# Hybrid decoder layer: attention values as the stationary operand, results by features, sample key sums in four column groups

## Chip, cores and metric

The kernel runs on one core of one Trainium2 chip. The metric is the device time of one execution in microseconds. The core's engines are named as the profile names them: PE is TensorE (matmuls; PEld is its weight load), DVE is VectorE, ACT is ScalarE, POOL is GpSimd, SP is SyncE, which here issues DMAs.

## The reference

One layer of a decoder trunk and a last norm, for a prompt of 512 tokens and 8 sample sequences of one token each, which share the weights. Cut to what matters here:

```
u = RMSNorm(x)
[qA,kA,vA | qB,kB,vB,rB,gate_lowrank | gate_A,gate_B] = u @ w_in
A: dilated sliding-window softmax attention, 3 head groups x 4 heads x 64 dims,
   (window, dilation) = (128,1),(512,4),(2048,16); for each head slot the three groups' outputs
   are merged, weighted by their softmax denominators -> 256 wide
   samples: one query against the cached keys and values of each group
B: gated linear attention (GLA), 4 heads, dk=128, dv=256:
   S_t = diag(a_t) S_{t-1} + k_t^T v_t, o_t = q_t S_t, RMSNorm per head, swish gate -> 1024 wide
mix = sigmoid(gate_A) * (oA @ w_pa) + sigmoid(gate_B) * (oB @ w_pb);   x = x + mix @ w_o
x = x + relu(RMSNorm(x) @ w_up)^2 @ w_down
```

Of the change only two pieces of A are touched: the products of probabilities and values of the prompt, with the merge of the groups, and the sum over cached positions of probabilities times values of the samples.

## The kernel before

Activations are kept by features: 128 features on the partitions, 520 columns for 512 prompt tokens and 8 samples, in two halves of 260. The weights come in panels of 1024 x 128. Each panel is loaded by SP (`raw`), split by ACT into a rounded high part (`whi`, L90) and by DVE into the rest (`wlo`, L91); two half panels each, four buffers. The panel loop (L124, tile `mps`) multiplies high by high, high by low and low by high: 8 slices x 3 passes x 2 halves, 48 matmuls of 128 x 128 by 260. Most of PE's time is this loop, through the panels of w_in, w_pa (2), w_pb, w_o, w_up and w_down.

Everything else is filler between the panels. The parts are generators: prompt attention (`attn`, from L311), the samples' attention (`attn_s`, L402), the GLA heads of the prompt (`gla`, L548), and the samples' states (`gla_s`, L662). Between two panels `fill` (L130) advances them by one to four steps, and at the end `finish` (L143) drains what is left. GLA's generators begin only when both attention generators are done (`gla_parts`, L828). The order in which the instructions come out of this is then arranged by the framework's scheduler with a timeline of its own, so a change in one filler moves others. All fillers share four PSUM banks (`bank`, L66).

*Prompt attention* works through two sides, the direct group (`on`) and the two dilated groups (`oc`), each in four blocks of 128 queries. A block computes scores (`sps`, L332), exponentials (L340) with their minima and sums in `stN` and `stC`, transposes of the probabilities (`ptp`, L347), and their product with the values (`pvp`, L358). In that product the transposed probabilities are the stationary operand, 128 x 128, and 64 columns of values of one head move; the result stands by tokens. At the end, the weights of the two sides are worked out from exchanged minima and sums (`cz`, L375 to L383), the two results are multiplied by them (L385), transposed to features (`oT`, L391 and L396) and added into `oa` (L393, L398).

*Samples' attention* multiplies the cached values by the probabilities in place (`kcb`, L472), adds the groups, and sums over the 128 cached positions on the partitions (`spO`): 16 matmuls with a 128 x 128 piece of `kcb` as the stationary operand and a single column of ones moving. They are put on a list (`small_mm`, L154) and taken from it between the steps of the panel loop or by `finish` (L151). DVE then copies the result (L484).

*A GLA head* computes decays (`zp`, L554), scaled keys and their transposes (`klp`, L575, copied by ACT as `klT`, L577), then six levels of a triangular product (`lev`, L545, L610, L615) whose factors `D` take two exponentials on ACT each (L604, L605) and have three buffers, then POOL's copies into `ST` (L626), the state matmuls (`gpo`, `gpu`, L632 to L636), a norm, and transposes of the result (`gop`, L656). The samples' states are loaded in pairs, split by ACT and POOL into high and low (L701, L702) and multiplied (`gso`, L706).

Behind the panels of the two gates, ACT computes their sigmoids over all 4160 columns at once (gA at L871, gB at L872), with a table load before and behind. Then come the two w_pa panels (stationary w_pa, moving `oas`) and the w_pb panels, which need the GLA result split into `obh` and `obl` (L741).

Of the kernel before, what the change touches and what calls it, by code (L numbers as in the profile page):

```python
# [9 lines left out]
F32 = mybir.dt.float32  # L10
F32R = mybir.dt.float32r
U8 = mybir.dt.uint8
AF = mybir.ActivationFunctionType
ALU = mybir.AluOpType
# [4 lines left out]
D = 1024  # L19
S = 512  # L20
NB = 8
P = 128
HC = 260
NT = 2 * HC
# [6 lines left out]
def pv(t):  # L31

    return t[:, :, :256]
# [11 lines left out]
class Build:  # L45
# [265 lines left out]
    def attn(self, ap):  # L311
        nc = self.nc
        on, oc, prTs = self.on, self.oc, self.prTs
        stN = ap.tile([P, 4, 2, 4], F32, tag="stN", name="stN", bufs=1)
        stC = ap.tile([P, 4, 2, 4], F32, tag="stC", name="stC", bufs=1)
        K, Q, V = self.KTt, self.QTt, self.Va
        for side, (o, st, mk) in enumerate(((on, stN, self.c["maskN"]), (oc, stC, self.c["maskC"]))):
            while side == 1 and self.groups_ready < 3:
                yield True
            for b in range(4):  # L320
                first = 1 if side == 0 and b == 0 else 0
                pss = [self.bank("sps").rearrange("p (h x) -> p h x", h=2) for _ in range(2)]
                for hp in range(2):
                    for hh in range(2):
                        rows = slice(64 * hh, 64 * hh + 64)
                        if side == 0:
                            nc.tensor.matmul(pss[hh][:, hp, first * P:], Q[rows, hp, b * P:(b + 1) * P],
                                             K[rows, hp, (b - 1 + first) * P:(b + 1) * P], start=True, stop=True)
                        else:
                            for gg in range(2):  # L330
                                i = 2 + 2 * gg + hp
                                nc.tensor.matmul(pss[hh][:, hp, gg * P:(gg + 1) * P], Q[rows, i, b * P:(b + 1) * P],  # L332
                                                 K[rows, i, b * P:(b + 1) * P], start=True, stop=True)
                prs = [ap.tile([P, 2, 256], F32, tag="pr", name="pr", bufs=3) for _ in range(2)]
                for h in range(4):
                    pr = prs[h // 2]
                    nc.vector.tensor_tensor_reduce(
                        pr[:, h % 2, first * P:], pss[h % 2][:, h // 2, first * P:], mk[:, first * P:], scale=-0.125,
                        scalar=3.0e38, op0=ALU.add, op1=ALU.min, accum_out=st[:, b, 0, h:h + 1])
                    nc.scalar.activation(pr[:, h % 2, first * P:], pr[:, h % 2, first * P:], AF.Exp, scale=-1.0,  # L340
                                         bias=st[:, b, 0, h:h + 1], accum_out=st[:, b, 1, h:h + 1])
                yield
                for hp in range(2):
                    pt = self.bank("ptp").rearrange("p (h x q) -> p h x q", h=2, x=2)
                    for hh in range(2):
                        for x in range(first, 2):
                            nc.tensor.transpose(pt[:, hh, x], prs[hp][:, hh, x * P:(x + 1) * P], self.c["ident"])  # L347
                    prT = prTs[hp].rearrange("p (h x q) -> p h x q", h=2, x=2)
                    nc.scalar.activation(prT[:, :, first:], pt[:, :, first:], AF.Copy)
                    po = self.bank("pvp")  # L350
                    for hh in range(2):
                        h = 2 * hp + hh
                        for x in range(first, 2):
                            if side == 0:
                                v = V[:, b - 1 + x, h * 64:h * 64 + 64]
                            else:
                                v = V[:, b, 256 * (x + 1) + h * 64:256 * (x + 1) + h * 64 + 64]
                            nc.tensor.matmul(po[:, hh * 64:hh * 64 + 64], prT[:, hh, x], v,  # L358
                                             start=(x == first), stop=(x == 1))
                    nc.vector.tensor_copy(o[:, b, hp * P:(hp + 1) * P], po[:, :P])  # L360
                    yield
        dN = self.dp.tile([S, 8], F32, tag="dN", name="dN")
        dC = self.dp.tile([S, 8], F32, tag="dC", name="dC")
        nc.gpsimd.dma_start(dN.rearrange("(b p) s -> p b s", p=P), stN.rearrange("p b a h -> p b (a h)"))
        nc.gpsimd.dma_start(dC.rearrange("(p r) s -> p r s", r=4), stC.rearrange("p b a h -> p b (a h)"))
        xN = ap.tile([P, 4, 2, 4], F32, tag="xN", name="xN", bufs=1)
        xC = ap.tile([P, 4, 2, 4], F32, tag="xC", name="xC", bufs=1)
        nc.gpsimd.dma_start(xN.rearrange("p b a h -> p b (a h)"), dC.rearrange("(b p) s -> p b s", p=P))
        nc.gpsimd.dma_start(xC.rearrange("p b a h -> p b (a h)"), dN.rearrange("(p r) s -> p r s", r=4))
        yield  # L370
        for st, xt, o in ((stN, xN, on), (stC, xC, oc)):
            m = ap.tile([P, 4, 4], F32, tag="cm", name="cm", bufs=2)
            w = ap.tile([P, 2, 4, 4], F32, tag="cw", name="cw", bufs=2)
            z = ap.tile([P, 4, 4], F32, tag="cz", name="cz", bufs=2)
            nc.vector.tensor_tensor(m, st[:, :, 0], xt[:, :, 0], op=ALU.min)  # L375
            nc.vector.tensor_tensor(w[:, 0], m, st[:, :, 0], op=ALU.subtract)
            nc.vector.tensor_tensor(w[:, 1], m, xt[:, :, 0], op=ALU.subtract)
            nc.scalar.activation(w, w, AF.Exp)
            nc.vector.tensor_tensor(z, w[:, 0], st[:, :, 1], op=ALU.mult)
            nc.vector.tensor_tensor(m, w[:, 1], xt[:, :, 1], op=ALU.mult)  # L380
            nc.vector.tensor_tensor(z, z, m, op=ALU.add)
            nc.vector.reciprocal(z, z)
            nc.vector.tensor_tensor(z, z, w[:, 0], op=ALU.mult)  # L383
            ov = o.rearrange("p b (h d) -> p (b h) d", h=4)
            nc.vector.tensor_tensor(ov, ov, z.rearrange("p b h -> p (b h)").unsqueeze(2).to_broadcast([P, 16, 64]),  # L385
                                    op=ALU.mult)
            yield
        for hp in range(2):
            pt = self.bank("oT")
            for b in range(4):  # L390
                nc.tensor.transpose(pt[:, b * P:(b + 1) * P], on[:, b, hp * P:(hp + 1) * P], self.c["ident"])  # L391
            oav = halves(self.oa[:, hp])
            nc.vector.tensor_copy(pv(oav), pt.rearrange("p (j c) -> p j c", j=2))  # L393
            p2 = self.bank("oT2")
            for b in range(4):
                nc.tensor.transpose(p2[:, b * P:(b + 1) * P], oc[:, b, hp * P:(hp + 1) * P], self.c["ident"])  # L396
            ovc = pv(oav).rearrange("p j (i r) -> p j i r", r=4)
            nc.vector.tensor_tensor(ovc, p2.rearrange("p (r j i) -> p j i r", r=4, j=2), ovc, op=ALU.add)  # L398
            yield


    def attn_s(self, ap):  # L402
        nc, I = self.nc, self.I
# [4 lines left out]
        for gi in range(3):  # L408
# [8 lines left out]
            for hp in range(2):  # L417
                nc.tensor.transpose(pq[:NB, hp * P:(hp + 1) * P], self.QTt[:, 2 * gi + hp, S:], self.c["ident"])
            qt = ap.tile([NB, 256], F32, tag="qt", name="qt", bufs=1)
# [7 lines left out]
                                    op=ALU.add)  # L427
# [7 lines left out]
        for gi in range(3):  # L435
            for hp in range(2):
                nc.tensor.matmul(pS[:32, gi * NB:(gi + 1) * NB], qf[:, gi, hp], kn[:, 2 * gi + hp],
                                 start=(hp == 0), stop=(hp == 1))
# [4 lines left out]
        st = ap.tile([32, 4], F32, tag="sst", name="sst", bufs=1)  # L443
# [30 lines left out]
                nc.vector.tensor_tensor(self.kcb[0], self.kcb[0], self.kcb[1], op=ALU.add)  # L474
            yield
        po = self.bank("spO")
        for i in range(16):
            b, hp = i // 2, i % 2
            self.small_mm(po[:, 8 * hp + b:8 * hp + b + 1], self.kcb[0][:, P * i:P * i + P], self.ones[:, 0:1],
                          start=True, stop=True)  # L480
        nc.vector.tensor_tensor(og[:, 2], sl[:, :, 0], sl[:, :, 1], op=ALU.add)
        nc.vector.tensor_tensor(og[:, 2], og[:, 2], sl[:, :, 2], op=ALU.add)
        yield from self.drain_tiny()
        nc.vector.tensor_copy(og[:, 3], po[:, :16].rearrange("p (x b) -> p x b", x=2))  # L484
        for hp in range(2):
            nc.vector.tensor_tensor(sv(halves(self.oa[:, hp])), og[:, 3, hp].rearrange("p (j c) -> p j c", j=2),
                                    og[:, 2, hp].rearrange("p (j c) -> p j c", j=2), op=ALU.add)
# [265 lines left out]
    def run(self):  # L753
# [33 lines left out]
        self.KTt, self.QTt = kt[:, :6], qt[:, :6]  # L787
        kt, qt, va = (t.rearrange("p a b -> p (a b)") for t in (kt, qt, va))
        self.Va = va[:, :4 * 768].rearrange("p (a b) -> p a b", a=4)
        self.on, self.oc = (t[:, 6 * NT:6 * NT + D].rearrange("p (b f) -> p b f", b=4) for t in (kt, qt))  # L790
        self.prTs = [va[:, 3072 + 512 * i:3584 + 512 * i] for i in range(2)]
        rp, aps, gps, gss = (ExitStack() for _ in range(4))
        right = dict(bufs=1, side="right")
# [342 lines left out]
```

## Time and profile before

| | us |
|---|---|
| Median of 3 runs | 969.25 (967.69 to 971.42) |
| Profiled execution, time | 968.6 |
| Profiled execution, span | 966.8 |
| PE busy | 928.8 |
| DVE busy | 556.5 |
| ACT busy | 389.8 |
| POOL busy | 102.3 |

The span is what the hardware profiler recorded between the first and the last instruction; the time of the same execution has 1.8 us more around it. An engine's busy time counts its instructions, not its waits. A row of the timeline gives the start and the length in us, then the engine, the line, the operation, the tile written and the tiles read, the shape, and how many records the row joins; brackets give the idle time in front of it and what ended it. PE's records overlap, so what one costs is read from start to start. A plain fp32 matmul leaves two records (transposes one), a matmul of the panel loop one. A row of the table by stretch gives the stretch, its length, the busy times of PE, PEld, DVE, ACT and POOL with the number of records, PE's granted clock (1.00 is full speed), the DMA share and GB/s.

### The profile page before, as it was taken

How to read it: one execution, taken by the hardware profiler on the slowest of the kernel's cores; microseconds unless marked ns; L12 is line 12 of the kernel's file. 1: busy time of each engine (PE TensorE's matmuls, PEld its weight loads, DVE VectorE, ACT ScalarE, POOL GpSimd, SP SyncE). 2: the span in 40 equal slices, each digit the busy share in tenths (PEclk: the TensorE clock that was granted, in tenths of full speed). 3: DMA queues.
4: the chain of work that ended last, by engine and by line, in shares of the span. 5: the costliest groups of instructions: out<-in, count | busy, mean ns of one | idle time of the engine just before them, and what ended most of it. 6: DMA issues, size and time to landing. Idle time of an engine off the chain costs nothing.

```text
span 966.8 us, 19936 instructions
## 1 busy us (share of the span) xinstructions
PE 928.8 (96%) x8288; PEld 909.0 (94%) x8288; DVE 556.5 (58%) x1075; ACT 389.8 (40%) x760; POOL 102.3 (11%) x148
## 2 busy tenths in 40 slices
PE   6999999999998999899899999999999999999994
PEld 6999999999898988789899999999999999999993
DVE  6657747645866946748665556443443344555654
ACT  6233243352644545556633444422432243224532
POOL 1000000001323322311000000010000000000000
PEclk9999999998999999899999999999999999999997
DMA  7455735322445344211468776778775222323311
GB/s 237 149 200 201 227 114 189 111 66 70 154 133 180 116 149 147 78 53 64 160 240 305 261 262 218 278 265 306 262 261 197 88 87 90 108 88 109 110 46 44
DMA packets 38988, 155.28 MB, mean 161 GB/s; under 512 B 5561, under 2 KB 11969, under 8 KB 36946
## 3 DMA queue, kind: packets, MB, share of 16 engines
q1 hardware_dynamic: 33778, 95.26, 28.7%
q0 software_dynamic: 4976, 58.74, 17.7%
q8 instruction: 65, 1.06, 0.5%
q14 instruction: 25, 0.20, 0.1%
q10 hardware_dynamic: 144, 0.01, 0.0%
HBM read 140.66 MB, written 54.17 MB: 202 GB/s over the span
## 4 chain that ended last, share of the span: by engine, by line
PE 83%; DMA 5%; DVE 4%; issue 3%; POOL 2%; ACT 2%; SPq 0%; DVEq 0%; POOLq 0%; ACTq 0%
PE mps L124 69%; PE mps L968 5%; PE pvp L358 1%; DMA svb<-dV 1%; DMA sst<-in_state 1%; POOL gx L702 1%; DMA raw<-in_w_in 1%; PE ptp L347 1%; DMA QTt<-ro 1%; DMA out_sgla<-sst 1%; PE spO L151 1%; PE vps L298 1%; DVE wlo L91 1%; POOL out_sgla L708 1%; PE sps L332 0%
## 5 line engine op out<-in xcount | busy, mean ns | idle before, releaser
L90 ACT ACTIVATE whi<-raw 128x512 fp32r<-128x512 f32 x264 | 165.7, 629 | 361.3 <-PE mps L124 309.7
L91 DVE TENSOR_TENSOR wlo<-raw,whi 128x512 fp32r<-128x512 f32 x264 | 184.8, 701 | 148.9 <-ACT whi L90 147.3
L124 PE MATMUL mps<-uh,whi 128*128 128x260 f32 x928 | 194.4, 289 | 7.4 <-ACT whi L90 5.5
L124 PE MATMUL mps<-ul,whi 128*128 128x260 f32 x928 | 195.8, 290 | 0.0
L124 PE MATMUL mps<-uh,wlo 128*128 128x260 f32 x928 | 193.2, 288 | 0.0
L124 PEld LDWEIGHTS mps<-uh,whi 128*128 128x128 f32 x928 | 145.8, 191 | 8.4 <-ACT whi L90 5.5
L124 PEld LDWEIGHTS mps<-ul,whi 128*128 128x128 f32 x928 | 146.5, 191 | 2.6 <-issue 1.4
L124 PEld LDWEIGHTS mps<-uh,wlo 128*128 128x128 f32 x928 | 146.2, 191 | 1.8 <-issue 1.1
L124 PE MATMUL mps<-hh,whi 128*128 128x260 f32 x512 | 103.2, 283 | 0.0
L124 PE MATMUL mps<-hh,wlo 128*128 128x260 f32 x512 | 103.2, 283 | 0.0
L124 PE MATMUL mps<-hl,whi 128*128 128x260 f32 x512 | 103.0, 283 | 0.0
L124 PEld LDWEIGHTS mps<-hh,whi 128*128 128x128 f32 x512 | 79.0, 188 | 0.1
L124 PEld LDWEIGHTS mps<-hh,wlo 128*128 128x128 f32 x512 | 78.9, 188 | 0.0
L124 PEld LDWEIGHTS mps<-hl,whi 128*128 128x128 f32 x512 | 78.7, 188 | 0.0
L124 PE MATMUL mps<-fh,wlo 128*128 128x260 f32 x384 | 77.3, 283 | 0.0
L124 PE MATMUL mps<-fl,whi 128*128 128x260 f32 x384 | 77.2, 283 | 0.0
L124 PE MATMUL mps<-fh,whi 128*128 128x260 f32 x384 | 76.8, 282 | 0.0
L124 PEld LDWEIGHTS mps<-fh,wlo 128*128 128x128 f32 x384 | 59.2, 188 | 0.0
L124 PEld LDWEIGHTS mps<-fl,whi 128*128 128x128 f32 x384 | 59.0, 188 | 0.0
L124 PEld LDWEIGHTS mps<-fh,whi 128*128 128x128 f32 x384 | 59.0, 188 | 0.0
L968 PE MATMUL mps<-fh,lw 128*128 128x260 f32 x256 | 46.6, 283 | 0.0
L968 PEld LDWEIGHTS mps<-fh,lw 128*128 128x128 f32 x256 | 39.6, 188 | 0.1
(330 smaller groups left out, 1377.6 us busy)
## 6 DMA issues: line engine op xcount, KB each, us to landing
raw<-in_w_in SPq DMA_DIRECT2D x57, 512.0 KB, 3.6
raw<-in_w_up SPq DMA_DIRECT2D x32, 512.0 KB, 4.2
raw<-in_w_down SPq DMA_DIRECT2D x32, 512.0 KB, 4.6
sst<-in_state SPq DMA_DIRECT2D x16, 256.0 KB, 2.7
svb<-dV SPq DMA_DIRECT2D x16, 256.0 KB, 3.5
out_sgla<-sst POOLq DMA_DIRECT2D x16, 256.0 KB, 3.7
raw<-in_w_pb SPq DMA_DIRECT2D x8, 512.0 KB, 4.4
raw<-in_w_o SPq DMA_DIRECT2D x8, 512.0 KB, 5.7
```

The source lines that it names most:

```text
L90: nc.scalar.activation(hi, raw[:, x:x + n], AF.Copy)
L91: nc.vector.tensor_tensor(lo, raw[:, x:x + n], hi.bitcast(F32), op=ALU.subtract)
L124: self.last = nc.tensor.matmul(out[j], w, x[:, k, j * HC:(j + 1) * HC], start=(k == 0 and n == 0), stop=(k == kt - 1 and n == 2))
L151: self.nc.tensor.matmul(*args, **kw)
L298: nc.tensor.transpose(pt[:, r * P:(r + 1) * P], vt[:, r * P:(r + 1) * P], self.c["ident"])
L347: nc.tensor.transpose(pt[:, hh, x], prs[hp][:, hh, x * P:(x + 1) * P], self.c["ident"])
L358: nc.tensor.matmul(po[:, hh * 64:hh * 64 + 64], prT[:, hh, x], v, start=(x == first), stop=(x == 1))
L702: nc.gpsimd.tensor_tensor(lo, st, hi.bitcast(F32), op=ALU.subtract)
L708: nc.gpsimd.dma_start(O["sgla"][2 * bp:2 * bp + 2, h].rearrange("b d v -> d b v"), st)
L968: nc.tensor.matmul(ps, w, x[:, kk, cc], start=(kk == 0 and n == 0), stop=(kk == KT - 1 and n == 2))
```

## The change

Four things are rewritten.

- Value product: the values, 64 columns of one head, are now the stationary operand and the transposed probabilities move, 128 columns. The two heads of a pair write the two halves of the partitions (column groups of 64), and are issued in turn. The result stands by features, so `on` and `oc` are laid out as [feature, pair, token].
- Merge: the results are not scaled by tokens any more. Instead each weight `cz` is spread over 64 columns (`zx`, one buffer, a copy of 512 columns on DVE) and transposed (`zT`, 4 x 4 transposes, as many as `oT` had), and the two sides are multiplied by it by features, then added.
- Key sums: 32 columns of ones are the stationary operand, and 512 columns of `kcb` move, in four matmuls that write four groups of 32 partitions. ACT copies the 128 x 512 result into `kcb`'s second half, four transposes (`spV`) turn it, and DVE picks every 32nd column.
- The sums are issued as ordinary matmuls and not through the list of small ones.

```diff
                     po = self.bank("pvp")
-                    for hh in range(2):
-                        h = 2 * hp + hh
-                        for x in range(first, 2):
+                    for x in range(first, 2):
+                        for hh in range(2):
+                            h = 2 * hp + hh
...
-                            nc.tensor.matmul(po[:, hh * 64:hh * 64 + 64], prT[:, hh, x], v,
+                            nc.tensor.matmul(po[64 * hh:64 * hh + 64, :P], v, prT[:, hh, x],
                                              start=(x == first), stop=(x == 1))
-                    nc.vector.tensor_copy(o[:, b, hp * P:(hp + 1) * P], po[:, :P])
+                    nc.vector.tensor_copy(o[:, hp, b * P:(b + 1) * P], po[:, :P])
...
-            ov = o.rearrange("p b (h d) -> p (b h) d", h=4)
-            nc.vector.tensor_tensor(ov, ov, z.rearrange("p b h -> p (b h)").unsqueeze(2).to_broadcast([P, 16, 64]),
-                                    op=ALU.mult)
+            zs.append(z)
             yield
         for hp in range(2):
-            pt = self.bank("oT")
-            for b in range(4):
-                nc.tensor.transpose(pt[:, b * P:(b + 1) * P], on[:, b, hp * P:(hp + 1) * P], self.c["ident"])
+            pts = []
+            for z in zs:
+                pt = self.bank("zT")
+                zx = ap.tile([P, 4, 2, 64], F32, tag="zx", name="zx", bufs=1)
+                nc.vector.tensor_copy(zx, z[:, :, 2 * hp:2 * hp + 2].unsqueeze(3).to_broadcast([P, 4, 2, 64]))
+                for b in range(4):
+                    nc.tensor.transpose(pt[:, b * P:(b + 1) * P], zx[:, b].rearrange("p h d -> p (h d)"),
+                                        self.c["ident"])
+                pts.append(pt)
             oav = halves(self.oa[:, hp])
-            nc.vector.tensor_copy(pv(oav), pt.rearrange("p (j c) -> p j c", j=2))
-            p2 = self.bank("oT2")
-            for b in range(4):
-                nc.tensor.transpose(p2[:, b * P:(b + 1) * P], oc[:, b, hp * P:(hp + 1) * P], self.c["ident"])
+            nc.vector.tensor_tensor(pv(oav), on[:, hp].rearrange("p (j c) -> p j c", j=2),
+                                    pts[0].rearrange("p (j c) -> p j c", j=2), op=ALU.mult)
+            nc.vector.tensor_tensor(oc[:, hp], oc[:, hp], pts[1], op=ALU.mult)
             ovc = pv(oav).rearrange("p j (i r) -> p j i r", r=4)
-            nc.vector.tensor_tensor(ovc, p2.rearrange("p (r j i) -> p j i r", r=4, j=2), ovc, op=ALU.add)
+            nc.vector.tensor_tensor(ovc, oc[:, hp].rearrange("p (r j i) -> p j i r", r=4, j=2), ovc, op=ALU.add)
...
         po = self.bank("spO")
-        for i in range(16):
-            b, hp = i // 2, i % 2
-            self.small_mm(po[:, 8 * hp + b:8 * hp + b + 1], self.kcb[0][:, P * i:P * i + P], self.ones[:, 0:1],
-                          start=True, stop=True)
+        for i in range(4):
+            nc.tensor.matmul(po[32 * i:32 * i + 32, :512], self.ones[:, :32], self.kcb[0][:, 512 * i:512 * i + 512],
+                             start=True, stop=True)
+        ov = self.kcb[1][:, :512]
+        nc.scalar.activation(ov, po, AF.Copy)
...
-        yield from self.drain_tiny()
-        nc.vector.tensor_copy(og[:, 3], po[:, :16].rearrange("p (x b) -> p x b", x=2))
+        yield
+        pt = self.bank("spV")
+        for y in range(4):
+            nc.tensor.transpose(pt[:, y * P:(y + 1) * P], ov[:, y * P:(y + 1) * P], self.c["ident"])
+        nc.vector.tensor_copy(og[:, 3].rearrange("p x (i c) -> p x c i", c=2),
+                              pt.rearrange("p (c x u) -> p x c u", c=2, x=2)[:, :, :, 0::32])
```

The new code shifts the lines behind it: by 4 or 5 in the merge and by 11 behind the samples' attention.

**How it moves instructions.** First PE around the key sums (a row gives line, operation, tiles, and shape). Before, they stand behind the scores of the last block of dilated attention:

```order
L358 MATMUL pvp<-Va 128x64 x4
L332 MATMUL sps<-KTt,QTt 128x128 x8
L151 MATMUL spO<-ones,kcb 128x1 x16
L347 MATMUL ptp<-ident,pr 128x128 x2
L124 MATMUL mps<-uh,wlo 128x260
L347 MATMUL ptp<-ident,pr 128x128 x2
L124 MATMUL mps<-uh,wlo 128x260
```

Now they stand ahead of the scores of the block before that one, with their own transposes `spV` behind:

```order
L358 MATMUL pvp<-Va 64x128 x4
L484 MATMUL spO<-kcb,ones 32x512 x4
L332 MATMUL sps<-KTt,QTt 128x128 x8
L124 MATMUL mps<-ul,whi 128x260 x2
L124 MATMUL mps<-uh,wlo 128x260 x2
L124 MATMUL mps<-uh,whi 128x260 x2
L124 MATMUL mps<-ul,whi 128x260 x2
L124 MATMUL mps<-uh,wlo 128x260
L493 MATMUL spV<-ident,kcb 128x128 x4
```

That is 86 projection matmuls earlier, and 9 projection matmuls now stand between the sums and their transposes. The transposes of the merge, which before stood in one row of twelve behind a first group of four, stand in four groups with 24, 30 and 29 projection matmuls between them. All of GLA follows later: `zp` of heads 0 to 3 stands behind 111, 120, 118 and 121 more projection matmuls than before, and the key transposes `klp` of heads 2 and 3 behind 147 and 123 more.

Second, ACT at the end of the gate panels. Before, head 3's exponentials (`D`) are all ahead of the split of `obh` and the sigmoid of gB:

```order
L604 ACTIVATE D<-D 128x64x4
L605 ACTIVATE D<-D 128x64x4
L90 ACTIVATE whi<-raw 128x512
L604 ACTIVATE D<-D 128x128x2
L605 ACTIVATE D<-D 128x128x2
L741 ACTIVATE obh<-R 128x520 x6
L90 ACTIVATE whi<-raw 128x512 x3
L643 ACTIVATE os<-gpo 128x256
L645 ACTIVATE jk,ssq<-gpo 128x256
L872 ACT_TABLE_LOAD
L872 ACTIVATE gB<-gB 128x4160
L873 ACT_TABLE_LOAD
```

Now the copy of `klT` and the exponentials of the last four levels are behind both:

```order
L90 ACTIVATE whi<-raw 128x512
L752 ACTIVATE obh<-R 128x520 x6
L883 ACT_TABLE_LOAD
L883 ACTIVATE gB<-gB 128x4160
L884 ACT_TABLE_LOAD
L588 ACTIVATE klT<-klp 128x512
L615 ACTIVATE D<-D 128x16x16
L616 ACTIVATE D<-D 128x16x16
L615 ACTIVATE D<-D 128x32x8
L616 ACTIVATE D<-D 128x32x8
L615 ACTIVATE D<-D 128x64x4
L616 ACTIVATE D<-D 128x64x4
```

Third, PE at the same place. Before, the last levels of head 3 stand among gate panels (moving `uh`, `ul`), well ahead of the first w_pa matmul:

```order
L124 MATMUL mps<-uh,wlo 128x260 x2
L124 MATMUL mps<-uh,whi 128x260
L545 MATMUL lev<-D 32x32 x16
L124 MATMUL mps<-uh,whi 128x260
L124 MATMUL mps<-ul,whi 128x260 x2
```

Now four levels in one piece stand behind 48 w_pa matmuls (moving `oas`), and the state matmuls follow without a projection matmul between them:

```order
L124 MATMUL mps<-oas,wlo 128x260 x2
L124 MATMUL mps<-oas,whi 128x260 x4
L124 MATMUL mps<-oas,wlo 128x260 x2
L556 MATMUL lev<-D 32x32 x64
L643 MATMUL gpo<-Vb,ST 128x256
L647 MATMUL gpu<-Vb,klT 128x256
L643 MATMUL gpo<-Vb,ST 128x256
L647 MATMUL gpu<-Vb,klT 128x256
L643 MATMUL gpo<-Vb,ST 128x256
L645 MATMUL gpo<-state,qe 128x256
```

In both orders 12 more w_pa matmuls stand between the first two and the last six transposes of head 3's result, and the rest of the program is the same behind these.

More of the change, by code (lines that the diff above doesn't have):

```diff
@@ L370, in attn @@
         yield
-        for st, xt, o in ((stN, xN, on), (stC, xC, oc)):
+        zs = []
+        for st, xt in ((stN, xN), (stC, xC)):
             m = ap.tile([P, 4, 4], F32, tag="cm", name="cm", bufs=2)
@@ L789, in run @@
         self.Va = va[:, :4 * 768].rearrange("p (a b) -> p a b", a=4)
-        self.on, self.oc = (t[:, 6 * NT:6 * NT + D].rearrange("p (b f) -> p b f", b=4) for t in (kt, qt))
+        self.on, self.oc = (t[:, 6 * NT:6 * NT + D].rearrange("p (x t) -> p x t", x=2) for t in (kt, qt))
         self.prTs = [va[:, 3072 + 512 * i:3584 + 512 * i] for i in range(2)]
```

## The prediction

> **What bounds the kernel now.** I read the page's first part, then the chain that ended last, then the two groups that the change rewrites, then TensorE's timeline and busy time by stretch.
>
> ```profile
> PE 928.8 (96%) x8288; PEld 909.0 (94%) x8288; DVE 556.5 (58%) x1075; ACT 389.8 (40%) x760; POOL 102.3 (11%) x148
> ...
> PE 83%; DMA 5%; DVE 4%; issue 3%; POOL 2%; ACT 2%; SPq 0%; DVEq 0%; POOLq 0%; ACTq 0%
> ```
>
> TensorE is busy for 928.8 of 966.8 us and makes up 83% of the chain. So a step counts if it takes TensorE time, changes its clock, or opens or closes one of the few holes. VectorE and ScalarE (58% and 40%) matter only where TensorE waits for them. Those places are late: the gated-linear-attention (GLA) stage, and above all its end.
>
> The two rewritten groups, by tile, the attention-times-values product and the samples' key sums:
>
> ```profile
> L358 PE MATMUL pvp<-Va x120: 217/275/275, 72.0 to 234.5; 128*128 128x64 f32 x120
> ...
> L151 PE MATMUL spO<-ones,kcb x32: 250/352/353, 219.4 to 224.6; 128*128 128x1 f32 x32
> ```
>
> Each matmul of plain fp32 leaves two records, so these are 60 and 16 matmuls. What they cost is read from start to start on TensorE's timeline, since the durations overlap:
>
> ```profile
> 219.40 5.51 PE L151 MATMUL spO<-ones,kcb 128*128 128x1 f32 x32
> 224.77 0.67 PE L347 MATMUL ptp<-ident,pr 128*128 128x128 f32 x2
> ...
> 229.05 0.40 PE L124 MATMUL mps<-uh,whi 128*128 128x260 f32 x2
> 229.29 0.28 PE L124 MATMUL mps<-ul,whi 128*128 128x260 f32 x1
> 229.41 1.00 PE L358 MATMUL pvp<-Va 128*128 128x64 f32 x8
> 230.25 0.61 PE L347 MATMUL ptp<-ident,pr 128*128 128x128 f32 x4
> ```
>
> A projection matmul (mps) takes 0.12 us (two from 229.05 to 229.29). A group of four value matmuls takes 0.84 us (229.41 to 230.25). The key sums take 5.37 us (219.40 to 224.77).
>
> **The change, part by part.**
>
> *1. Value matmuls, 60 of them, 14 groups of four and 2 of two.* The stationary side shrinks from 128 columns to 64 and the moving side grows from 64 to 128, so the work halves only if the two heads' column groups run side by side. No row of before has a 64-column group. The nearest are the 32-column groups of GLA's levels, and the price of moving columns comes from two fp32 matmuls:
>
> ```profile
> 263.82 0.28 PE L124 MATMUL mps<-uh,whi 128*128 128x260 f32 x1
> 264.03 0.46 PE L545 MATMUL lev<-D 128*32 128x32 f32 x32
> 264.42 0.39 PE L124 MATMUL mps<-uh,whi 128*128 128x260 f32 x1
> 264.64 0.40 PE L124 MATMUL mps<-ul,whi 128*128 128x260 f32 x2
> ...
> 423.64 0.59 PE L632 MATMUL gpo<-Vb,ST 128*128 128x256 f32 x2
> 424.07 0.59 PE L636 MATMUL gpu<-Vb,klT 128*128 128x256 f32 x2
> ```
>
> One matmul with 256 moving columns takes 0.43 us, two records, so 0.215 for 256 columns and 0.107 for 128. The 32 level records of 32 columns would take 32 x 0.027 = 0.86 us one after the other; they took 0.39, so several ran together. With four together they need 0.21, and 0.18 is left for entering the other layout. The matmul ahead took 0.21 and the one behind 0.22 where 0.12 is usual, 0.19 more. A change of layout and back thus costs about 0.37 us. A new group is 4 slots x 0.107 = 0.43, plus 0.37: 0.80 against 0.84. Over 14 groups that is -0.6. A group of two took half of 0.84 and will take 0.21 + 0.37 = 0.58: +0.3 for the pair. Five groups are followed at once by scores or key sums, which have a layout of their own, so there a share of the switch is paid already, about -0.2 each. Term: **-1.0 us**. Ends: without any switching cost -0.41 x 14 - 0.2 x 2 = -6.1; with the heads one after the other (0.86 + 0.37 = 1.23) +0.39 x 14 + 0.4 x 2 = +6.3.
>
> The Trainium skill, "TensorEngine Tiling (Array Packing)", section Tiling Modes, Key Properties, speaks against the change here: "Mode switching requires drain", since between projection matmuls each group pays it twice. The trace agrees, as the 0.21 and 0.22 us beside 0.12 show; by the same list's independent tiles alone the term would be -6.1, and with the drain it is -1.0.
>
> *2. Key sums.* The 16 matmuls with one moving column become 4 with 512 columns in four column groups, plus one ScalarE copy and four transposes. Two stretches of TensorE's table (busy us of PE, PEld, DVE, ACT, POOL, then the granted clock):
>
> ```profile
> 219.40:224.77 5.37, 5.37 (x33) 5.37 (x33) 1.47 (x8) 2.08 (x8) 1.12 (x2) 0.65 0.18 68
> 224.77:228.10 3.33, 3.33 (x18) 3.33 (x18) 1.06 (x9) 0.60 (x1) 0.19 (x1) 0.53 0.06 7
> 395.10:402.00 6.90, 6.07 (x90) 5.55 (x91) 4.33 (x11) 1.64 (x4) 2.45 (x2) 0.51 0.23 78
> 415.60:419.00 3.40, 3.40 (x45) 3.34 (x34) 3.40 (x11) 1.27 (x2) 0.00 (x0) 0.50 0.16 27
> 449.81:469.18 19.37, 17.82 (x334) 16.94 (x333) 15.02 (x35) 9.77 (x22) 2.34 (x5) 1.00 0.21 70
> 469.18:484.60 15.42, 13.29 (x92) 12.13 (x90) 11.47 (x26) 11.01 (x19) 0.59 (x1) 1.00 0.54 198
> ```
>
> In the key sums the clock falls to 0.65, and in the 3.33 us behind them it is 0.53. That stretch holds 12 projection matmuls and 4 transposes, which at full clock take 12 x 0.12 + 4 x 0.11 = 1.9, so 1.4 us more is lost. After the change: four side by side are 2 slots x 0.43 = 0.86, entering 0.1, and four transposes 0.44: 1.4. Term: 1.4 - 5.4 - 1.4 = **-5.4 us**. Ends: one after the other (8 x 0.43 = 3.4, so 4.0 in all) -2.8; with the transposes hidden -6.0. The ScalarE copy costs nothing as long as projection matmuls cover it: by the order, a group of scores and 9 of them stand between the sums and the transposes. A copy of 512 columns, as ScalarE does for each half panel, is over by then; without this cover it would be about 0.6 us.
>
> *3. Merge of the two attention sides.* Two passes of 1024 columns and two copies leave VectorE; four copies and two multiplications come. The transposes stay sixteen. VectorE is busy for 58%, so the difference itself is nothing. But the spread factors pass through one buffer, so the four groups of transposes stand some 30 projection matmuls apart by the order, and GLA waits until attention is done. GLA's first step of heads 0 to 3 now follows 111, 120, 118 and 121 more projection matmuls, head 3's key transposes 123 more, about 14 us of projections. Filler that stands later among them costs nothing; what counts is what becomes of TensorE's holes, in the middle and at the end.
>
> *4. The middle.* Holes on TensorE, in brackets the idle time and its releaser, and the gate's sigmoid on ScalarE:
>
> ```profile
> 384.77 0.29 PE L706 MATMUL gso<-gx 128*16 128x256 f32 x1 [1.17 <-ACT gx L701]
> 389.34 0.29 PE L706 MATMUL gso<-gx 128*16 128x256 f32 x1 [1.18 <-ACT gx L701]
> 392.50 0.52 PE L706 MATMUL gso<-gx 128*16 128x256 f32 x3 [1.20 <-POOL gx L702]
> 395.93 1.12 PE L575 MATMUL klp<-ident,kl 128*128 128x128 f32 x4 [1.95 <-POOL kl L572]
> 414.72 0.46 PE L545 MATMUL lev<-D 128*32 128x32 f32 x32 [1.49 <-DVE D L607]
> ...
> 406.77 3.68 ACT L871 ACTIVATE gA<-gA 128x4160 f32<-128x4160 f32 x1
> ```
>
> These five waits are 7.0 us, and the stretches at clock 0.51 and 0.50 hold 6.07 and 3.40 busy us, of which half, 4.7, is lost to the clock: 11.7 in all. In the new order 57 projection matmuls (before 24) stand ahead of the second half of head 3's sample states, 23 (before 8) between them and the key transposes of head 2, and the sigmoid of gA comes while TensorE has those. I expect two thirds of it gone: **-7.5 us**. Ends: 0 (the waits, which end on state loads and their splits, come up elsewhere) and -11.
>
> *5. The end of the gates.* Here the delay is paid. T is 469.18, the first matmul behind the gate panels (w_pa).
>
> ```profile
> 464.48 0.46 PE L545 MATMUL lev<-D 128*32 128x32 f32 x32
> ...
> 469.18 0.64 PE L124 MATMUL mps<-oas,whi 128*128 128x260 f32 x4
> ...
> 454.39 0.42 ACT L604 ACTIVATE D<-D 128x256 f32<-128x256 f32 x1 [3.15 <-DVE D L602]
> ...
> 462.74 3.28 ACT L741 ACTIVATE obh<-R 128x520 fp32r<-128x520 f32 x6 [0.56 <-DVE D L607]
> ...
> 469.19 0.64 ACT L90 ACTIVATE whi<-raw 128x512 fp32r<-128x512 f32 x1 [2.13 <-PE mps L124]
> ...
> 472.83 3.68 ACT L872 ACTIVATE gB<-gB 128x4160 f32<-128x4160 f32 x1
> 476.52 1.28 ACT L873 ACT_TABLE_LOAD   x1
> ...
> 465.39 1.27 POOL L626 COPY ST<-sd 32x128 f32<-32x128 f32 x4 [14.38 <-DVE sd L623]
> ```
>
> Before, all of head 3's levels were done at T, and 60 w_pa matmuls (7.2 us) with the state matmuls covered gB's sigmoid; from T to the last head's transposes were 15.42 us. Now only the key transposes and the first levels come near T. ScalarE's order is a panel split that waits for a buffer until T (+0.64), the split of obh (3.28), a table (1.28), the sigmoid (3.68), a table (1.28), klT (0.6): T + 10.8. Behind them stand the exponentials of the last four levels. From such a first exponential to the last level's matmuls took 10.1 us before (454.39 to 464.48), among panel work; here VectorE is free, and I take 7.4: T + 18.2. Mask, the POOL copies (1.27) and handing over: T + 20.5. Eleven state matmuls of 0.43: T + 25.3. The normalisation's small steps, some 2.7: T + 28.0; transposes and the last 12 covering matmuls: T + 30.2. TensorE's cover, 48 w_pa matmuls and the early levels, is used up near T + 9. This is 14.8 us more than 15.42. Against it stands head 3's work that left the stretch before T: 19.37 us there held 112 projection matmuls (13.4), so 5.9. That leaves +8.9. TensorE will also be nearly idle for some 10 us, and the two stretches of the middle went to half clock behind waits of 1.95 and 1.49; up to 3 us more, most of which I take. Term: **+11.5 us**. Ends: +6 (levels in 5 us, full clock), +14.5 (levels in 10.1, half clock).
>
> **Sum.** -1.0 - 5.4 - 7.5 + 11.5 = -2.4 on the profiled run's 968.6 (its span 966.8 and 1.8 around it): 966.2. The median shown, 969.25, is about 0.6 above that run: **966.8 us**.
>
> **Rivals.** *R1, slower: ScalarE's queue at the end decides.* The levels wait behind gB's sigmoid in full at half clock (+14.5) and the middle gains only 2: 968.6 - 6.4 - 2 + 14.5 + 0.6 = 975.3. It decides as soon as the end costs more than 6.4 plus the middle's gain. For it: the order of ScalarE is fixed, and 9.5 us of it stand ahead of klT. Against: all five holes of the middle end on work that gets more cover. *R2, faster: the end is short.* Levels in 5 us at full clock (+6), middle -9: 968.6 - 6.4 - 9 + 6 + 0.6 = 959.8. For it: exponentials of 0.4 and a VectorE without panel work. Against: three buffers for the levels, which also held back the last one before. *R3: the column groups do not run side by side,* so that the change does not do what it says: +6.3, -2.8, -7.5, +11.5: 976.7. Against it: 0.39 us for 32 level records.
>
> **How the numbers follow.** Forecast 0.45, R1 0.22, R2 0.27, R3 0.06. A measurement of this kernel can tell about 0.5%, 4.8 us: faster is below 964.4, slower above 974.1. R2 and a fifth of the forecast's spread are faster: 0.36. R3 and most of R1 are slower: 0.23. The rest, 0.41, is the same. The range takes in R2 with the value matmuls at 3 us less, and R1 and R3: 957 to 977.
>
> **What would show it.** In the changed profile: a value group from start to start at 0.80 us (0.43 without a switch, 1.2 serial); the key sums near 1 us, and no slice below 0.9 of clock there; fewer holes between 384 and 419; the last levels' exponentials behind gB's sigmoid, with TensorE empty for some 10 us behind the gate panels. I am wrong if that hole is under 5 us, or the middle's waits come back.

## The result, and the profile after

The changed kernel takes 977.85 us (median of 5 runs, 975.95 to 978.71) against 969.25 (967.6 to 971.5): ratio 1.0083, 95% interval 1.0060 to 1.0107. In a second batch of runs the ratio was 1.0052 (1.0029 to 1.0076). So it is slower by 0.5 to 0.8%, where the forecast was 966.8 us within 957 to 977, slightly faster. The range is missed by only 0.9 us, and 1.0052 times 969.25 would be 974.3, inside it; the direction is wrong in both batches.

First the page of the changed kernel, then two tiles, then TensorE's timeline at the key sums and at a value group, then one stretch there (busy us of PE, PEld, DVE, ACT, POOL, then the granted clock):

```profile
PE 926.7 (95%) x8268; PEld 900.0 (92%) x8268; DVE 556.0 (57%) x1079; ACT 392.4 (40%) x763; POOL 99.2 (10%) x148
```

```profile
L358 PE MATMUL pvp<-Va x120: 272/273/324, 72.3 to 235.4; 128*64 128x128 f32 x120
...
L484 PE MATMUL spO<-kcb,ones x8: 592/604/617, 206.8 to 207.2; 128*32 128x512 f32 x8
```

```profile
206.77 1.06 PE L484 MATMUL spO<-kcb,ones 128*32 128x512 f32 x8
207.77 1.26 PE L332 MATMUL sps<-KTt,QTt 64*128 64x128 f32 x16
...
230.55 0.28 PE L124 MATMUL mps<-uh,whi 128*128 128x260 f32 x1
230.76 0.66 PE L358 MATMUL pvp<-Va 128*64 128x128 f32 x8
231.35 0.66 PE L347 MATMUL ptp<-ident,pr 128*128 128x128 f32 x4
```

```profile
206.80:211.10 4.30, 4.30 (x44) 3.34 (x43) 2.27 (x10) 2.27 (x7) 0.00 (x0) 1.00 0.38 122
```

Both rewritten products do what they should: the key sums take 1.00 us from start to start (5.37 before) at full clock, a value group 0.59 (0.84 before), with 0.21 for the panel matmul ahead of it, where 0.12 is usual. The time is lost elsewhere. At the end of the gate panels:

```profile
458.63 0.64 PE L124 MATMUL mps<-oas,whi 128*128 128x260 f32 x4
...
463.90 0.41 PE L124 MATMUL mps<-oas,wlo 128*128 128x260 f32 x2
471.05 1.21 PE L124 MATMUL mps<-oas,whi 128*128 128x260 f32 x4 [6.74 <-DVE gA L896]
...
476.43 1.05 PE L556 MATMUL lev<-D 128*32 128x32 f32 x96
479.40 0.51 PE L556 MATMUL lev<-D 128*32 128x32 f32 x32 [1.92 <-DVE D L618]
481.65 1.22 PE L643 MATMUL gpo<-Vb,ST 128*128 128x256 f32 x2 [1.74 <-POOL ST L637]
...
491.43 0.44 PE L667 MATMUL gop<-ident,os 128*128 128x128 f32 x2 [2.38 <-DVE os L662]
```

On VectorE at that place, and on ScalarE:

```profile
463.48 2.52 DVE L753 TENSOR_TENSOR obl<-R,obh 128x520 fp32r<-128x520 f32 x4
...
469.48 0.69 DVE L753 TENSOR_TENSOR obl<-R,obh 128x520 fp32r<-128x520 f32 x1
470.20 0.70 DVE L896 TENSOR_TENSOR gA<-mps,gA 128x520 f32<-128x520 f32 x1
```

```profile
464.64 3.67 ACT L883 ACTIVATE gB<-gB 128x4160 f32<-128x4160 f32 x1
...
470.11 0.41 ACT L615 ACTIVATE D<-D 128x256 f32<-128x256 f32 x1
```

```profile
464.30:471.05 6.75, 0.01 (x2) 0.04 (x1) 6.67 (x15) 6.71 (x8) 0.00 (x0) 0.88 0.24 78
471.05:476.43 5.38, 5.38 (x25) 5.24 (x25) 3.29 (x9) 0.99 (x4) 0.00 (x0) 0.52 0.00 0
```

TensorE is empty for 6.75 us, with 24 of the 48 w_pa matmuls ahead of the levels still to do: the results of the first 24 lie in PSUM and wait for VectorE's product with gA, which stands behind the split of `obl` and the levels' subtractions (L613, three in VectorE's queue between 466.1 and 469.6). The rest then runs at clock 0.52.

The panel loop leaves 6752 records in every run, so its n-th record is the same place in every kernel. Between such places (us, from the traces' record starts):

| kernel | ratio to before (95%) | 0 to 912 | 912 to 1584, attention | 1584 to 2816, GLA | 2816 to 2880, end | 912 to 2880 |
|---|---|---|---|---|---|---|
| before, first profile | 1 | 130.7 | 114.5 | 218.5 | 16.0 | 349.0 |
| before, second profile | 1.0023 (0.9990 to 1.0055) | 135.7 | 114.5 | 218.8 | 16.0 | 349.2 |
| changed, first profile | 1.0083 (1.0060 to 1.0107) | 134.6 | 104.8 | 213.5 | 35.8 | 354.1 |
| changed, second profile | 1.0052 (1.0029 to 1.0076) | 133.5 | 104.8 | 212.4 | 35.3 | 352.5 |
| e1_sums | 0.9990 (0.9961 to 1.0020) | 133.9 | 109.5 | 220.0 | 17.5 | 347.0 |
| e2_values | 1.0033 (1.0001 to 1.0064) | 133.8 | 109.7 | 220.4 | 19.5 | 349.6 |
| e3_four_buffers | 1.0046 (1.0018 to 1.0074) | 135.4 | 107.4 | 228.2 | 17.5 | 353.1 |
| e4_two_buffers | 1.0033 (1.0005 to 1.0062) | 135.8 | 106.0 | 219.6 | 23.9 | 349.5 |
| e5_sigmoid | 1.0092 (1.0056 to 1.0128) | 133.7 | 104.8 | 212.4 | 36.7 | 353.8 |
| e6_split | 1.0030 (1.0011 to 1.0048) | 135.5 | 104.8 | 214.6 | 33.8 | 353.2 |
| e7_both | 1.0011 (0.9987 to 1.0034) | 137.5 | 104.8 | 212.9 | 30.9 | 348.6 |
| e8_delay | 1.0122 (1.0089 to 1.0155) | 133.4 | 113.2 | 217.6 | 27.9 | 358.8 |
| e9_gA | 1.0061 (1.0036 to 1.0086) | 135.5 | 104.9 | 212.6 | 35.0 | 352.5 |
| e10_combined | 0.9957 (0.9938 to 0.9977) | 133.4 | 106.2 | 216.8 | 19.6 | 342.5 |

The first 912 records differ by 7 us from run to run, in the same kernel by 5; behind them two profiles of one kernel agree within 1.6. So the kernels are read from 912 on: attention gains 9.7 us, GLA 5 to 6, and the end loses 19.5. Each ratio is to runs of before in the same batch; e1 to e4 ran on one chip, the second profiles and e5 to e10 on another. The kernel before against itself gave 1.0023, so a ratio that near to 1 says little, and the stretches decide. A stretch is known from one profile of each experiment.

### The profile page after: what moved, and what is told of

The parts are those of the page before. It is cut to its first block, busy times and chain, and to the rows that moved or that the text cites. A ratio compares the mean times of both kernels' runs of the same rounds, so it can differ in the third digit from the quotient of the medians.

```text
span 976.1 us, 19908 instructions
## 1 busy us (share of the span) xinstructions
PE 926.7 (95%) x8268; PEld 900.0 (92%) x8268; DVE 556.0 (57%) x1079; ACT 392.4 (40%) x763; POOL 99.2 (10%) x148
## 4 chain that ended last, share of the span: by engine, by line
PE 52%; DVE 3%; issue 2%; DMA 1%; ACT 1%; POOL 1%; DVEq 0%; ACTq 0%; POOLq 0%; SPq 0%
PE mps L124 45%; PE mps L979 5%; DMA out_sgla<-sst 1%; PE gpo L643 1%; PE gpu L647 0%; DVE cum L571 0%; POOL qe L578 0%; DVE wlo L91 0%; DVE D L613 0%; PE gpo L645 0%; DMA sst<-in_state 0%; ACT L548 0%; DVE el L577 0%; DVE dd L996 0%; PE gop L667 0%
## 5 line engine op out<-in xcount | busy, mean ns | idle before, releaser
L91 DVE TENSOR_TENSOR wlo<-raw,whi 128x512 fp32r<-128x512 f32 x264 | 186.9, 709 | 158.2 <-ACT whi L90 155.7
```

Source lines behind the costliest of these rows:

```text
L91: nc.vector.tensor_tensor(lo, raw[:, x:x + n], hi.bitcast(F32), op=ALU.subtract)
```

## The experiments

**The parts alone, and the delay taken out.** Three questions: which part loses, and does the loss go when GLA is brought back to its place.

e1_sums is the kernel before with the new key sums, e2_values with all the rest of the change:

```diff
 e1_sums, against before:
-            self.small_mm(po[:, 8 * hp + b:8 * hp + b + 1], ...
+            nc.tensor.matmul(po[32 * i:32 * i + 32, :512], self.ones[:, :32], ...
 e2_values, against the changed kernel:
-            nc.tensor.matmul(po[32 * i:32 * i + 32, :512], self.ones[:, :32], ...
+            self.small_mm(po[:, 8 * hp + b:8 * hp + b + 1], ...
```

> The kernel before with the new key sums alone; value product and merge are the old ones. By its order GLA starts 36 projection matmuls later than before, but head 3's key transposes only 2 later, and all exponentials of head 3 stay ahead of gB's sigmoid. Theory A (the loss of the changed kernel is the end of the gates, which the merge delays): the sums' gain of 5.4 us stays whole, 963 to 965. Theory B (the new matmul forms or the steps around them cost more than they save, wherever GLA stands): no gain, 968 or more. Theory C (any delay of GLA is paid): 965 to 967.

> The kernel before with the new value product and merge alone; key sums as before. By its order GLA starts 75 projection matmuls later, head 3's key transposes 39 later; all exponentials of head 3 stand ahead of the split of obh and of the sigmoid, one level behind 10 matmuls of w_pa. Theory A: value product -2, early waits +2, a small piece of the end, 968 to 973. Theory B (the value product is what is slow): all the loss of 8.6 and the sums' gain that hid a part of it, 980 or more. Theory C: about half of the delay's price, 974 to 978.

e4_two_buffers has two buffers for the spread weights; e3_four_buffers has these two and the two `prTs` tiles:

```diff
-                zx = ap.tile([P, 4, 2, 64], F32, tag="zx", name="zx", bufs=1)
+                zx = ap.tile([P, 4, 2, 64], F32, tag="zx", name="zx", bufs=2)
 e3_four_buffers, for hp = 1 instead:
+                zx = prTs[len(pts)].rearrange("p (b h d) -> p b h d", b=4, h=2)
```

> The changed kernel with four places for the spread weights (two buffers, and the two tiles of transposed probabilities, which are free by then) in place of one. By its order head 3 stands where it stood before: key transposes 0 later, last level among the gate panels, exponentials ahead of the sigmoid. Value product, key sums and the merge's arithmetic are those of the changed kernel. Theory A: the end costs what it did before, so 969 - 2 - 5 + 2: 962 to 966, some 13 us under the changed kernel. Theory B: the loss stays, 974 to 978. Theory C: 963 to 967, as A.

> The changed kernel with two buffers for the spread weights. By its order head 3's key transposes are 67 projection matmuls later than before (123 in the changed kernel), the last level alone stands behind the sigmoid of gB and behind 48 matmuls of w_pa. Theory A: three of the four late levels are covered again, most of the end's price of 19 is gone, 964 to 970. Theory B: 974 to 978. Theory C (the price goes with the delay): half of it, 969 to 973.

Measured: ratios 0.9990, 1.0033, 1.0046, 1.0033. Times 969.25 that is 968.3, 972.4, 973.7 and 972.5 us: e1_sums came out where theory B put it, e2_values where A did, e4_two_buffers where C did, and e3_four_buffers in no stated range, 0.3 us under B's. So the times alone do not choose between the theories. The stretches do. Theory B falls: where the new matmuls stand time is gained, and attention gains 5.0 with the sums alone, 4.8 with the values alone and 9.7 with both (some of it is work that moved behind the place of reading). Theory A is right for the end: 17.5, 19.5, 17.5 and 23.9 us, longer as head 3 stands later. It is wrong for the whole. The gain does not stay: in e1_sums GLA takes 1.5 us more than before, and in e3_four_buffers, which has the end back, 9.7 more. The profile of e3_four_buffers, a run of 977.4 among runs from 969.3 to 978.6, has two new waits there on TensorE:

```profile
268.42 0.29 PE L718 MATMUL gso<-gx 128*16 128x256 f32 x1 [3.38 <-ACT gx L713]
273.33 0.82 PE L718 MATMUL gso<-gx 128*16 128x256 f32 x3 [3.19 <-POOL gx L714]
```

Both end on the split of a loaded sample state. So bringing GLA forward moved the loss from the end to the middle. No run tried what lengthened that chain; the trace leads both waits back to held-up instructions on VectorE and GpSimd (last section).

**Both kernels again.** Nothing is changed here.

> The kernel before again, for a second profile of it. The first batch showed single runs of one kernel spread over 10 us, and all four kernels some 3 us behind the first profile of before already at the 624th projection matmul, also the one whose instructions are the same up to there. Theory N (that is run to run, outside the change): this profile is 2 to 4 us behind the first one at that place too, the median equals that of before. Theory O (the orders differ in some way that counts): it equals the first profile there.

> The changed kernel again, on one chip with the kernels beside it. Ratio to before 1.006 to 1.011 as before. In its profile the first w_pa products wait over 5 us for VectorE's product with gA, and the stretch from the first w_pa matmul to the last transposes of head 3 is about 35 us, if the end is what costs; if it is the middle, that stretch varies and the middle is 8 us longer than in the kernel before.

Measured: theory N. The second profile of before is 5 us behind the first at the 912th record and 0.2 us from it in all that follows. The end of the changed kernel is 35.3 us again, with a wait of 6.75 for the product with gA, as expected; its ratio, 1.0052, is below the 1.006 to 1.011 that was expected.

**Which queue holds the end.** e5_sigmoid ties gB's sigmoid to head 3's last exponential, e6_split the split of `obl` to the fourth product with gA, e7_both has both.

```diff
 e5_sigmoid:
-        nc.scalar.activation(gB, gB, AF.Sigmoid)
+        c = nc.scalar.activation(gB, gB, AF.Sigmoid)
+        tc.add_manual_dep(c.ins, self.lastexp.ins.name, ...)
 e6_split:
-        self.split_big(self.R, obh, obl)
...
+                        self.lastga = nc.vector.tensor_tensor(o, i, o, op=ALU.mult)
+                    if x == 0 and k == 3:
+                        self.split_big(self.R, obh, obl, self.lastga)
```

> The changed kernel with one dependency more: gB's sigmoid waits for head 3's last exponential, so that klT's copy and the last four levels' exponentials stand ahead of it on ScalarE. Orders on TensorE and VectorE are those of the changed kernel. Theory S (what the prediction said: ScalarE's queue decides the end): 6 to 10 us under the changed kernel. Theory D (VectorE's queue decides: TensorE waits for the product with gA, which stands behind the split of obl and the levels' subtractions): TensorE's wait of 6.7 us stays, the levels come at once behind it, 1 to 4 us under the changed kernel.

> The changed kernel with only the split of obl moved behind the fourth product with gA on VectorE; gB's sigmoid stays ahead of head 3's last exponentials. Single runs differ by 5 us in the first 135 us whatever the kernel, so the stretch from the first w_pa products to the last transposes of head 3 is what is read: between the 2816th and the 2880th projection matmul 35.3 to 35.8 us in the changed kernel, 36.7 with the sigmoid behind, 30.9 with both. Theory D (VectorE's queue first): 31 to 33. Theory DS (two queues in a row, either alone is enough to hold the end): 34 to 36.

> As the one before, and besides the split of obl on VectorE is put behind the fourth product with gA. Theory S: as the one before, 6 to 10 us under the changed kernel, no more. Theory D: the wait for gA goes, 48 w_pa matmuls and the levels run side by side, 6 to 10 us under the changed kernel where the sigmoid alone gave 1 to 4.

Measured at the end: 36.7, 33.8 and 30.9 us, where the changed kernel has 35.3 to 35.8. TensorE's timeline of e5_sigmoid:

```profile
468.97 1.21 PE L124 MATMUL mps<-oas,whi 128*128 128x260 f32 x4 [6.75 <-DVE gA L900]
...
476.58 0.46 PE L556 MATMUL lev<-D 128*32 128x32 f32 x32 [1.92 <-DVE D L618]
...
483.14 0.70 PE L643 MATMUL gpo<-Vb,ST 128*128 128x256 f32 x2 [1.05 <-ACT jk L656]
```

of e6_split:

```profile
469.08 0.72 PE L124 MATMUL mps<-oas,whi 128*128 128x260 f32 x4 [3.21 <-DVE gA L900]
...
478.30 0.65 PE L556 MATMUL lev<-D 128*32 128x32 f32 x32 [1.66 <-DVE D L618]
```

Theory S falls: with the sigmoid out of the way the wait for VectorE stays at 6.75, and nothing is gained, where theory D had 1 to 4 us (the sigmoid now delays the copies behind the state matmuls). The split alone halves that wait and gives 1.7: 33.8 us lies between the 31 to 33 of theory D and the 34 to 36 of theory DS. Both together give 4.6, where D had said 6 to 10. So the two queues hold the end one behind the other, but they are the smaller part of it: with both orders 30.9 us are left, 14.9 more than before, of which 4 to 6 are head 3's work that came into the stretch. The rest goes with the late start of head 3, as 17.5 us in e3_four_buffers and 23.9 in e4_two_buffers show.

**The delay alone.** The kernel before, in which GLA's generators start four steps later and GLA's first instruction also waits for a later panel matmul; sums, values and merge are old.

```diff
+            for _ in range(4):
+                yield True
...
-            nc.gpsimd.memset(self.wg, 0.0)
+            c = nc.gpsimd.memset(self.wg, 0.0)
+            tc.add_manual_dep(c.ins, self.hist[-24].ins.name, ...)
```

> The kernel before, old value product, merge and key sums, with only one dependency more: GLA's first step waits for a projection matmul further on. By its order the key transposes of head 3 stand 96 projection matmuls later than before (changed kernel 123), two levels behind the split of obh, the last one behind gB's sigmoid. If the delay of GLA by itself is what costs: the stretch at the end 27 to 31 us (16.0 before), some 5 us of head 3's work gone ahead of it, and the whole 5 to 9 us slower than before. If the new matmul forms cost: the end stays near 16 to 20 and the whole within 2 us.

Measured: 982.79 us, ratio 1.0122; the end 27.9 us, the whole from 912 on 9.7 us longer. A row of its end:

```profile
478.75 0.73 PE L124 MATMUL mps<-oas,whi 128*128 128x260 f32 x4 [2.24 <-DVE gA L892]
```

The end is as expected, the whole more than the 5 to 9 us. This settles one point: a delay of GLA is enough for a loss of this size, without any of the new matmuls (the changed kernel loses 4.2 us from 912 on, and some 7 that it gained before). It does not show that the delay is the only way to lose: e3_four_buffers, without a delay of head 3, loses 4.0 there too.

**The middle.** e9_gA ties gA's sigmoid to the samples' last state split. First the waits of the changed kernel:

```profile
405.20 0.40 PE L717 MATMUL gso<-gx 128*16 128x256 f32 x1 [3.19 <-ACT gx L712]
413.31 0.66 PE L586 MATMUL klp<-ident,kl 128*128 128x128 f32 x4 [0.86 <-POOL kl L583]
```

The first wait ends on the split of a state, which stands behind gA's sigmoid on ScalarE in the changed kernel:

```profile
399.01 3.68 ACT L882 ACTIVATE gA<-gA 128x4160 f32<-128x4160 f32 x1
...
404.54 0.61 ACT L712 ACTIVATE gx<-sst 128x512 fp32r<-128x512 f32 x1
```

The edit of e9_gA:

```diff
-        nc.scalar.activation(gA, gA, AF.Sigmoid)
+        c = nc.scalar.activation(gA, gA, AF.Sigmoid)
+        tc.add_manual_dep(c.ins, self.lastgx.ins.name, ...)
```

> The changed kernel with gA's sigmoid behind the samples' last state split on ScalarE. In the changed kernel the state matmuls wait 2.9 to 3.3 us for that split, which stands behind the sigmoid and its tables. If that wait is what ate the middle's gain: it goes, and from the 1584th to the 2816th projection matmul 3 to 5 us are gained on 212.4 to 213.5. If the middle has its own length (state loads, the multiplications on GpSimd): another wait comes in its place and under 1 us is gained.

The waits in e9_gA:

```profile
397.97 0.29 PE L717 MATMUL gso<-gx 128*16 128x256 f32 x1 [1.38 <-ACT gx L712]
401.51 0.29 PE L717 MATMUL gso<-gx 128*16 128x256 f32 x1 [1.24 <-ACT gx L712]
411.69 0.67 PE L586 MATMUL klp<-ident,kl 128*128 128x128 f32 x4 [2.69 <-POOL kl L583]
```

The wait of 3.2 us goes, two of 1.4 and 1.2 come, the one for `kl` is 2.7 (0.86 and 2.10 in the two profiles of the changed kernel), and GLA takes 212.6 us as in the changed kernel (212.4 and 213.5). So the second expectation holds: the samples' chain has its own length here. Which link sets it (loads, splits, GpSimd) stays open.

**Together.** The changed kernel with two buffers for the spread weights and the two orders of e7_both.

> The changed kernel with two buffers for the spread weights, gB's sigmoid behind head 3's last exponential, and the split of obl behind the fourth product with gA. With two buffers alone the end took 23.9 us, and the whole was 1.0033 of before. If the two orders give here the 4.4 us that they gave in the changed kernel: the end 18 to 21, ratio to before 0.994 to 0.999. If the end is limited by head 3's chain itself: 22 to 25 and ratio 1.001 to 1.004.

Measured: 966.43 us (12 runs) against 971.31, ratio 0.9957 (0.9938 to 0.9977). It beats both kernels: from 912 on it takes 342.5 us, 6.6 less than before. Its end takes 19.6 us, where two buffers alone gave 23.9. The two orders were not tried in the kernel before.

```profile
466.34 0.46 PE L556 MATMUL lev<-D 128*32 128x32 f32 x32
466.73 0.75 PE L124 MATMUL mps<-oas,whi 128*128 128x260 f32 x4
...
468.74 0.70 PE L643 MATMUL gpo<-Vb,ST 128*128 128x256 f32 x2 [0.30 <-POOL ST L637]
```

The w_pa matmuls run without a wait, with the last level among them.

## Why the prediction was wrong

*Value matmuls and key sums* (-1.0 and -5.4): right. Attention is 9.7 us shorter. Of that, 2.7 us only moved behind the 1584th record (4 transposes of the merge 0.4, 8 of the values 1.1, the first steps of GLA's first head and of the samples 1.2; 1.9 at the prices of before), so 7.0 are gained and 6.4 were forecast. By e1_sums the sums gave 5.0 of it, which leaves 2.0 for the values. Between panel matmuls a value group costs 0.59 and some 0.1 on the panel matmuls on either side, 0.78 together, where the prediction had 0.80. The column groups run side by side: the eight records of the sums took 1.00 us, where eight of 0.43 make 3.4. Rival R3 is out. The sentence that no row of before has a 64-column group is wrong: one of the levels (L610) has such matmuls, eight records of 64 moving columns that took 0.68 us from start to start (452.28). They stand next to other small layouts, so they say little on the price of the switch.

*The middle* (-7.5): **this is the step that failed.** GLA is 5.7 us shorter between the places (means of two profiles). By the prediction's count 5.9 of head 3's work left that stretch, and 2.7 came into it, so the true gain is 2.5. The prediction added up five waits between 384 and 415 us and the half clock behind them, and took two thirds as gained because more projection matmuls stand there in the new order. All five did change. But a wait of 3.19 us behind gA's sigmoid took the place of three, and e9_gA shows that without it others come. All idle time of TensorE in the stretch fell only from 13.8 and 15.0 us to 11.7 and 10.9, and the mean granted clock, 0.977 and 0.984 before, is 0.984 in both profiles after, so a third of the half-clock time that the prediction read from one profile is not there in the other profile of the same kernel. This is nearer to the lower end of the term, "the waits come up elsewhere". It is also the prediction's own second sign of being wrong. What sets the length of the samples' chain stays open.

*The end* (+11.5): the late start of head 3 was seen, but the size is too small, and one cause was missed. The stretch grew by 19.5, less the 5.9: +13.6. The prediction let 48 w_pa matmuls cover up to T + 9 and saw ScalarE's queue as the only one. In the profile they stop at T + 5.7, since VectorE's products with gA, which free PSUM, stand behind the split of `obl`; the matmuls that should have been cover then ran at clock 0.52 ahead of the levels. By e5_sigmoid and e6_split neither queue alone frees the end.

*The 5.9 between the two terms* is too high. The row of that stretch has TensorE busy for 17.82 of 19.37 us, so 1.55 of the 5.9 was idle time. The records that moved to the end, 4 of `klp` and 216 of `lev`, took 0.53 and 3.34 us there. Counted by these 3.9, the middle gained 4.5 and the end cost 15.6, above the upper end of its term. The sum is the same, but the miss is then 3.0 in the middle and 4.1 at the end, where the prediction's count makes it 5.0 and 2.1. Both terms were too hopeful by either count.

*Sum:* -7.0 - 2.5 + 13.6 = +4.1, and from 912 to 2880 the kernel lost 4.2 (353.3 against 349.1, means of two profiles). The ratio of 1.0052 in the second batch says 5 us. The 8.6 us of the first batch hold some 4 more; the first profile of before had the shortest start of all fourteen (130.7 us), but whether the other runs of before in that batch shared it, these traces cannot say. Rival R1 came nearest in its sizes, with +14.5 at the end, a middle of -2, and 975.3 us. Its reason, ScalarE's queue alone, is refuted by e5_sigmoid, so there its number is in part luck.

## What to carry to other kernels

Where a bound engine lives on filler, a saving in one filler can be lost again where the chain behind it starts later: read where the last chain ends, and which engine's queue frees the buffers of the work that should cover it. e10_combined, whose head 3 starts late too, won once these queues were put in order. A group of waits that a new order seems to cover is better counted as kept, unless the chain that they end on becomes shorter; here most of it came back elsewhere.

## What was not expected of the hardware

In e3_four_buffers single instructions on VectorE and GpSimd grew by a factor of 4 to 10 while both worked:

```profile
255.83 4.20 DVE L618 TENSOR_TENSOR D<-D,QKb 128x256 f32<-128x256 f32 x1
259.95 0.41 DVE L619 TENSOR_TENSOR D<-D,QKb 128x256 f32<-128x256 f32 x1
```

```profile
255.95 1.30 POOL L584 TENSOR_TENSOR kl<-kl,QKb 128x512 f32<-128x512 f32 x1
257.20 2.53 POOL L714 TENSOR_TENSOR gx<-sst,gx 128x512 fp32r<-128x512 f32 x2
...
268.63 4.64 POOL L714 TENSOR_TENSOR gx<-sst,gx 128x512 fp32r<-128x512 f32 x1
```

The VectorE instruction took 4.20 us where the next of its form took 0.41, and ended right behind GpSimd's three (259.7); later one on GpSimd took 4.64 instead of 1.28, while VectorE was at work. Behind the first stood the split of a panel: SP's panel load waited 6.3 us for it and was issued at 261.66, the load of a state behind it in SP's queue at 262.08, and the first new wait of TensorE in this kernel (up to 268.42) ends on that state. The second (up to 273.33) ends on the long instruction of GpSimd. Such instructions are not special to this kernel: the second profile of before has one of 3.27 us on VectorE (261.82), and TensorE's longest wait in the 30 us behind it is 1.16. No run was made to isolate them.
